# Score products of 64 rows, two heads side by side, issued as one group per chunk with its own rank, in a hybrid decoder trunk

## The chip, the cores and the metric

The kernel runs on one core of a Trainium2 chip. The metric is the device time of one execution in microseconds (us). TensorE is PE in the profile (PEld is its weight load), VectorE DVE, ScalarE ACT, GpSimd POOL, SyncE SP; all loads and stores here are issued from SP's queue.

## The reference

Two layers over 16 meta tokens and 2048 tokens of width 1024, each wrapped in RMSNorms: an even layer (sliding-window attention beside a convolution module) and an odd layer, stick-breaking attention of 16 heads of 64, on which the change lies:

```python
for i in range(nb):
    kend = (i + 1) * BLOCK
    z = jnp.einsum('bqhd,bkhd->bhqk', qp[:, i * BLOCK:kend], kp[:, :kend]).astype(jnp.float32) * scale
    ...
    log_beta = jax.nn.log_sigmoid(z)
    log_1m = jnp.where(valid, jax.nn.log_sigmoid(-z), 0.0)
    after = lax.cumsum(log_1m, axis=3, reverse=True) - log_1m
    a = jnp.where(valid, jnp.exp(log_beta + after), 0.0)
    outs.append(jnp.einsum('bhqk,bkhd->bqhd', a.astype(v.dtype), vp[:, :kend]))
```

A weight is thus the sigmoid of the key's own score, times the product over all later keys of one minus theirs.

## The kernel before

The first part (`layer0`) is the even layer in four chunks of 512 tokens: projections, convolution on DVE, window attention, output projection. Its projections end in PSUM banks that `banks = cycle(BK)` takes in turn from the pools `pj` and `pz`; `pw` (L546) and `outp` (L645) take `pj` alone.

The second part (`layer1`) runs over eight head pairs p, for each the first eight query tiles (`attn(p, 0)`, the first half) and later all of the other eight (`attn(p, 1)`, the second half). `interleave` mixes the steps of `attn` with projection units of another head pair: a unit is 24 products (8 blocks of the width, each in three products of high and low parts, `mm3`, L142 to L144) into one bank. For a pair of query tiles (x = 0, 1) and the two heads (h = 0, 1), `pair_steps` cuts the keys into chunks of at most 512, from the last to the first. One `chunk`:

- For each of four tiles (h, x) the scores `z` (L912): q and k are split into a high and a low part of 64 rows each. The k tile of a head holds both parts above each other (128 rows), the q tile one part twice, so two products of 128 rows give all four terms.
- ACT takes two sigmoids, `om` (L919, of -z) and `be` (L920, of z); POOL masks the diagonal where needed (L923).
- DVE forms the running product of `om` from the right (the scan `S`, L925, that starts from the chunk before) and multiplies `be` by it (L926).
- PE transposes `be` block by block into a bank `pt` (L944), ACT copies it to `aT` (L947 to L950), and PE multiplies by v into `av` (L958), head 0 in the left half of the array's columns and head 1 in the right half. The first `av` of a chunk waits for all copies of the chunk (`after_all`).

The order on each engine is set by a scheduler that takes instructions by rank, normally the order of the code; `high_priority(offset=n)` moves a block n ranks forward (400 for `av`). Each engine then works strictly through its list. A chunk's last `av` is noted in `self.gates`; projections of layer 1 stand behind the fourth last of them (`behind`). The PSUM pools have 2 banks for `pj` (projections), 3 for `pz` (scores), 2 for `pt` and 1 for `av`.

The loads: `start` brings k (four loads per head pair) and v, `qload` brings q for a pair of query tiles (eight loads).

## Time and profile before

| | us |
|---|---|
| median of 3 runs | 2896.34 (2895.69 to 2900.71) |
| profiled execution | 2902.22 |
| its span, first to last instruction | 2900.5 |
| PE busy in the span | 2735.1 |
| DVE busy | 2209.4 |
| ACT busy | 1472.3 |
| scores (L912), 1536 products, busy | 394.9 |

Where the prediction quotes rows: a row of the timeline has start, duration, engine, line, operation, tiles, count, and in brackets the idle time before and what ended it. A group has count | busy time, mean duration in ns of one | idle time before, and its releasers. A row of the waits has who waited, for whom, the total, how often and the longest. A row of stretches has the stretch and its length, then for each engine the busy time and in brackets the instructions, then the granted clock of TensorE, the share of the DMA engines and GB/s. Durations of PE products include their way through the array, so products that follow each other overlap in the record, and a pitch is read from starts or ends.

### The profile page before, as it was taken

How to read it: one execution, taken by the hardware profiler on the slowest of the kernel's cores; microseconds unless marked ns; L12 is line 12 of the kernel's file. 1: busy time of each engine (PE TensorE's matmuls, PEld its weight loads, DVE VectorE, ACT ScalarE, POOL GpSimd, SP SyncE). 2: the span in 40 equal slices, each digit the busy share in tenths (PEclk: the TensorE clock that was granted, in tenths of full speed). 3: DMA queues.
4: the chain of work that ended last, by engine and by line, in shares of the span. 5: the costliest groups of instructions: out<-in, count | busy, mean ns of one | idle time of the engine just before them, and what ended most of it. 6: DMA issues, size and time to landing. Idle time of an engine off the chain costs nothing.

```text
span 2900.5 us, 49605 instructions
## 1 busy us (share of the span) xinstructions
PE 2735.1 (94%) x16110; PEld 2193.5 (76%) x16110; DVE 2209.4 (76%) x3696; ACT 1472.3 (51%) x3574; POOL 777.6 (27%) x2679
## 2 busy tenths in 40 slices
PE   7888999999899999999999899999999999999997
PEld 7886777777688799888887677777777777766876
DVE  7987888888767744666668987878888887887864
ACT  4223434343545323455445656666666766665551
POOL 3431212000000212333335532323223322333210
PEclk9999999999999999999999999999999999999999
DMA  7877888788876664444446462423232342244322
GB/s 258 283 251 221 254 267 256 234 241 267 235 209 187 213 199 146 130 127 137 128 137 182 130 178 65 113 76 101 66 103 88 88 111 73 74 129 126 113 95 91
DMA packets 303986, 462.87 MB, mean 160 GB/s; under 512 B 46640, under 2 KB 200640, under 8 KB 300656
## 3 DMA queue, kind: packets, MB, share of 16 engines
q1 hardware_dynamic: 303728, 459.70, 52.5%
q8 instruction: 129, 2.11, 0.3%
q14 instruction: 129, 1.06, 0.1%
HBM read 312.16 MB, written 142.14 MB: 157 GB/s over the span
## 4 chain that ended last, share of the span: by engine, by line
PE 71%; DVE 10%; DMA 7%; issue 4%; ACT 4%; POOL 2%; SPq 1%; DVEq 0%; ACTq 0%; POOLq 0%
PE pj L142 11%; PE pj L144 11%; PE pj L143 11%; PE z L912 8%; PE av L958 7%; PE pt L944 7%; PE po L142 4%; PE po L144 4%; PE po L143 4%; DVE y L309 3%; DVE S L925 2%; DMA qs<-qr 1%; DVE be L926 1%; DMA raw<-in_w_in 1%; ACT om L919 1%
## 5 line engine op out<-in xcount | busy, mean ns | idle before, releaser
L925 DVE TENSOR_TENSOR_SCAN S<-om,be 128x401 f32<-128x401 f32 (+3 forms) x512 | 536.6, 1069 | 71.9 <-ACT om L919 51.3
L919 ACT ACTIVATE om<-z 128x384 f32<-128x384 f32 (+5 forms) x768 | 377.9, 510 | 196.7 <-PE z L912 131.8
L926 DVE TENSOR_TENSOR be<-be,S 128x385 f32<-128x385 f32 (+5 forms) x768 | 413.6, 563 | 76.0 <-POOL be L917 22.2
L142 PE MATMUL pj<-th,wh 128*128 128x512 f32 (+2 forms) x1280 | 460.5, 360 | 7.1 <-DVE ev L810 3.6
L144 PE MATMUL pj<-th,wl 128*128 128x512 f32 (+2 forms) x1280 | 452.8, 354 | 0.0
L143 PE MATMUL pj<-tl,wh 128*128 128x512 f32 (+2 forms) x1280 | 450.5, 352 | 0.0
L950 ACT COPY aT<-pt 128x512 f32<-128x512 f32 (+2 forms) x672 | 334.2, 504 | 196.6 <-PE pt L944 156.2
L912 PE MATMUL z<-kst,qt 128*128 128x384 f32 (+6 forms) x1536 | 394.9, 357 | 31.2 <-ACT be L920 29.8
L920 ACT ACTIVATE be<-z 128x384 f32<-128x384 f32 (+5 forms) x768 | 375.5, 505 | 72.7 <-PE pt L944 72.0
L309 DVE SCALAR_TENSOR_TENSOR y<-u,cw,y 128x512 f32<-128x512 f32 (+1 forms) x480 | 391.7, 828 | 6.1
L944 PE MATMUL pt<-ident,be 128*128 128x128 f32 x2176 | 363.2, 282 | 17.4 <-ACT ev L799 7.7
L944 PEld LDWEIGHTS pt<-ident,be 128*128 128x128 f32 x2176 | 253.6, 142 | 113.0 <-issue 31.0
L912 PEld LDWEIGHTS z<-kst,qt 128*128 128x128 f32 x1536 | 247.7, 190 | 75.7 <-ACT be L920 55.3
L958 PE MATMUL av<-aT,vt 128*64 128x256 f32 (+1 forms) x2304 | 282.0, 380 | 4.3 <-DVE og L976 4.3
L916 POOL MEMSET om<- 128x1 f32 x768 | 74.8, 99 | 768.6 <-DVE S L925 753.5
L144 PE MATMUL pj<-hTh,wl 128*128 128x512 f32 (+2 forms) x704 | 246.7, 353 | 23.9 <-POOL wl L132 16.9
L142 PEld LDWEIGHTS pj<-th,wh 128*128 128x128 f32 x1280 | 241.8, 189 | 33.9 <-DVE ev L810 4.6
L144 PEld LDWEIGHTS pj<-th,wl 128*128 128x128 f32 x1280 | 241.0, 188 | 29.9
L143 PEld LDWEIGHTS pj<-tl,wh 128*128 128x128 f32 x1280 | 241.4, 189 | 25.1 <-issue 0.4
L142 PE MATMUL pj<-hTh,wh 128*128 128x512 f32 (+2 forms) x704 | 249.6, 356 | 8.9 <-DMA wh<-wk 4.6
L925 DVE TENSOR_TENSOR_SCAN S<-om 128x257 f32<-128x257 f32 (+4 forms) x256 | 204.8, 812 | 63.1 <-POOL om L923 50.3
L143 PE MATMUL pj<-hTl,wh 128*128 128x512 f32 (+2 forms) x704 | 246.8, 351 | 0.8 <-DVE hTl L191 0.8
(184 smaller groups left out, 4702.2 us busy)
## 6 DMA issues: line engine op xcount, KB each, us to landing
raw<-in_w_in SPq DMA_DIRECT2D x98, 512.0 KB, 4.0
wr<-wk SPq DMA_DIRECT2D x44, 512.0 KB, 6.2
wh<-wk SPq DMA_DIRECT2D x44, 512.0 KB, 5.2
wl<-wk SPq DMA_DIRECT2D x44, 512.0 KB, 6.5
qt<-qhd SPq DMA_DIRECT2D x256, 64.0 KB, 2.6
qt<-qld SPq DMA_DIRECT2D x256, 64.0 KB, 2.4
wk<-wh SPq DMA_DIRECT2D x22, 512.0 KB, 4.9
wk<-wl SPq DMA_DIRECT2D x22, 512.0 KB, 4.9
```

The costliest lines, as they stand in the source:

```text
L142: mm(out, sh, mh, start=first, stop=False)
L143: mm(out, sh, ml, start=False, stop=False)
L144: mm(out, sl, mh, start=False, stop=last)
L309: return lambda: nc.vector.scalar_tensor_tensor(y[:, :TC], u[:, w : w + TC], cw[:, j, w : w + 1], y[:, :TC], ALU.mult, ALU.add)
L912: nc.tensor.matmul(z[:, :n], S["q"][2 * h + i][:, x * P : x * P + P], S["k"][h][:, k0 : k0 + n], start=(i == 0), stop=(i == 1))
L919: nc.scalar.activation(om[:, :n], z[:, :n], AF.Sigmoid, scale=-0.125)
L920: nc.scalar.activation(be[:, :n], z[:, :n], AF.Sigmoid, scale=0.125)
L925: nc.vector.tensor_tensor_scan(P_[:, : n + 1][:, ::-1], om[:, : n + 1][:, ::-1], om[:, : n + 1][:, ::-1], init, ALU.mult, ALU.bypass)
L926: nc.vector.tensor_tensor(bl[:, : n + 1], bl[:, : n + 1], P_[:, : n + 1], ALU.mult)
L944: nc.tensor.transpose(pt[:, o : o + P], bes[h, x][:, mo + b * P : mo + b * P + P], self.ident)
L950: cps.append(nc.scalar.copy(aT[:, lo:hi], pt[:, lo:hi]))
L958: mi = nc.tensor.matmul(av[h * HD : h * HD + HD, qc0 + x0 : qc0 + 256], S["v"][:, b0 + b, h * HD : h * HD + HD], at, start=not S["started" ...
```

## The change

The scores become products of 64 rows. The k tiles now hold the high part of both heads above each other, and the low part; q likewise. So head 0 is in rows 0 to 63 and head 1 in rows 64 to 127, and three products (high by high, high by low, low by high) are made for each tile; low by low is left out. All scores of a chunk, up to 12 products into four banks, are issued ahead of its other work, with a rank 800 forward, and the first of them waits for the last sigmoids of the chunk before (`zread[-4:]`) and for the `aT` copies of its head 0 (`half`). The transposes run through head 0 first and then head 1. `pj` has 1 bank and `pz` 4; outside the stretches of attention the projections alternate between both.

```diff
-PB = (2, 3, 2)
+PB = (1, 4, 2)
+ZP = 800
...
-                    ps = self.bank("pj", "pw")
+                    ps = self.bank(next(banks), "pw")
...
+        self.zread, self.half, self.free = [], [], cycle(BK)
...
-                    ps = self.bank("pj", "pj1")
+                    ps = self.bank(next(self.free), "pj1")
...
-                for h in range(2):
+                for i in range(2):
                     kst = w4.tile([P, T], F32R, tag="kst", name="kst")
-                    for i in range(2):
-                        self.mv(kst[i * HD : i * HD + HD, :n], kd[i][p, h * HD : h * HD + HD, :n])
+                    self.mv(kst[:, :n], kd[i][p, :, :n])
                     ks.append(kst)
...
+                for i in range(2):
+                    qt = w2.tile([P, 256], F32R, tag=f"q{i}", name="qt")
+                    self.mv(qt, qd[i][p, :, q0 : q0 + 256])
+                    qs.append(qt)
...
+                    zs, wait = {}, self.zread[-4:] + self.half
+                    for x in range(2):
+                        n = nbs[x] * P + mo
+                        if n == 0:
+                            continue
+                        for h in range(2):
+                            zs[h, x] = self.bank("pz", "z")
+                        with tc.high_priority(offset=ZP):
+                            for i, j in ((0, 0), (0, 1), (1, 0)):
+                                for h in range(2):
+                                    r = slice(h * HD, h * HD + HD)
+                                    mi = nc.tensor.matmul(zs[h, x][:, :n], S["q"][i][r, x * P : x * P + P], S["k"][j][r, k0 : k0 + n], start=(i + j == 0), stop=(i == 1))
+                                    if wait is not None:
+                                        self.after_all(mi, wait)
+                                        wait = None
...
-                            z = self.bank("pz", "z")
-                            for i in range(2):
-                                nc.tensor.matmul(z[:, :n], S["q"][2 * h + i][:, x * P : x * P + P], S["k"][h][:, k0 : k0 + n], start=(i == 0), stop=(i == 1))
+                            z = zs[h, x]
...
-                            nc.scalar.activation(be[:, :n], z[:, :n], AF.Sigmoid, scale=0.125)
+                            self.zread.append(nc.scalar.activation(be[:, :n], z[:, :n], AF.Sigmoid, scale=0.125))
...
-                    for c in range(0, b1 - b0, 2):
-                        cw = min(2, b1 - b0 - c)
-                        aTs = []
-                        for h in range(2):
+                    cps, aTs = [], {}
+                    for h in range(2):
+                        for c in range(0, b1 - b0, 2):
+                            cw = min(2, b1 - b0 - c)
                             pt = self.bank("pt", "pt1")
...
+                        if h == 0:
+                            self.half = cps[:]
...
+        self.free = cycle(("pj",))
         for p in range(2, 6):
             interleave(proj(p, 0), attn(p - 2, 0))
...
+        self.free = cycle(BK)
         for t in range(8, NT):
```

How this moves PE's list in the second half, where three chunks follow each other in head pair 0. Before, the piece has the last transpose for head 0 of a chunk (`be_21300` is its x = 1), then the scores of head 0 for the second chunk after it (`z_21512`, `z_21525`, into whose `be` DVE comes two chunks later), then the `av` of the chunk before, and only then the first transpose of head 1 of the chunk itself (`be_21312`):

```order
L944 MATMUL pt1_21332<-ident_60,be_21300 128x128
L912 MATMUL z_21512<-kst_19877,qt_21102 128x400
L912 MATMUL z_21512<-kst_19877,qt_21105 128x400
L912 MATMUL z_21525<-kst_19877,qt_21102 128x400
L912 MATMUL z_21525<-kst_19877,qt_21105 128x400
L958 MATMUL av1_20627<-aT_21259,vt1_19883 64x256
L958 MATMUL av1_20627<-aT_21266,vt1_19883 64x256
L958 MATMUL av1_20627<-aT_21259,vt1_19883 64x256
L958 MATMUL av1_20627<-aT_21266,vt1_19883 64x256
L958 MATMUL av1_20627<-aT_21271,vt1_19883 64x256
L958 MATMUL av1_20627<-aT_21276,vt1_19883 64x256
L944 MATMUL pt1_21339<-ident_60,be_21312 128x128
```

So the scores of the next chunk were all issued by then, and those of the one after it have begun.

Now, at the same place, the four transposes into the first bank of head 1 of a chunk (`be_21321` is x = 0, `be_21330` is x = 1) stand directly ahead of the scores of the next one, of which these are the first eight (`z_21404` and `z_21412` are head 0, `z_21405` and `z_21413` head 1):

```order
L955 MATMUL pt1_21350<-ident_60,be_21321 128x128
L955 MATMUL pt1_21350<-ident_60,be_21330 128x128
L955 MATMUL pt1_21350<-ident_60,be_21321 128x128
L955 MATMUL pt1_21350<-ident_60,be_21330 128x128
L915 MATMUL z_21404<-kst_19861,qt_21104 128x512
L915 MATMUL z_21405<-kst_19861,qt_21104 128x512
L915 MATMUL z_21412<-kst_19861,qt_21104 128x512
L915 MATMUL z_21413<-kst_19861,qt_21104 128x512
L915 MATMUL z_21404<-kst_19863,qt_21104 128x512
L915 MATMUL z_21412<-kst_19863,qt_21104 128x512
L915 MATMUL z_21405<-kst_19863,qt_21104 128x512
L915 MATMUL z_21413<-kst_19863,qt_21104 128x512
```

No score of the next chunk stands ahead of a transpose that needs the last `be` of this one. The group's first four products alternate between the heads, the rest come by twos.

Right behind them, the last two scores of that group, the rest of head 1's transposes, then a transpose for head 0 of the next chunk (`be_21421`, whose scores are `z_21404`), and the `av` of the chunk itself:

```order
L915 MATMUL z_21405<-kst_19861,qt_21106 128x512
L915 MATMUL z_21413<-kst_19861,qt_21106 128x512
L955 MATMUL pt1_21357<-ident_60,be_21321 128x128
L955 MATMUL pt1_21357<-ident_60,be_21330 128x128
L955 MATMUL pt1_21456<-ident_60,be_21421 128x128
L971 MATMUL av1_20621<-aT_21343,vt1_19865 64x256
L971 MATMUL av1_20621<-aT_21355,vt1_19865 64x256
L971 MATMUL av1_20621<-aT_21343,vt1_19865 64x256
L971 MATMUL av1_20621<-aT_21355,vt1_19865 64x256
L971 MATMUL av1_20621<-aT_21348,vt1_19865 64x256
L971 MATMUL av1_20621<-aT_21360,vt1_19865 64x256
L955 MATMUL pt1_21463<-ident_60,be_21421 128x128
```

The `av` of a chunk has moved behind the first transpose of the next chunk; where a chunk has a projection unit, that too stands behind it, in two parts, ahead of the transposes of head 1.

More of the change, by code (lines that the diff above doesn't have):

```diff
@@ L644, in mm @@
                 w = slice(nh * 512, nh * 512 + 512)
-                ps = self.bank("pj", "po")
+                ps = self.bank(next(banks), "po")
                 for k in range(KB):
@@ L883, in qload @@
                 S["q"] = qs = []
-                for h in range(2):
-                    for i in range(2):
-                        qt = w2.tile([P, 256], F32R, tag=f"q{h}{i}", name="qt")
-                        for j in range(2):
-                            self.mv(qt[j * HD : j * HD + HD], qd[i][p, h * HD : h * HD + HD, q0 : q0 + 256])
-                        qs.append(qt)
+                for i in range(2):
+                    qt = w2.tile([P, 256], F32R, tag=f"q{i}", name="qt")
+                    self.mv(qt, qd[i][p, :, q0 : q0 + 256])
+                    qs.append(qt)
             def pair_steps(m):
@@ L909, in chunk @@
                                 continue
-                            z = self.bank("pz", "z")
-                            for i in range(2):
-                                nc.tensor.matmul(z[:, :n], S["q"][2 * h + i][:, x * P : x * P + P], S["k"][h][:, k0 : k0 + n], start=(i == 0), stop=(i == 1))
+                            z = zs[h, x]
                             om = w3.tile([P, 513], F32, tag="om", name="om")
@@ L930, in chunk @@
                             bes[h, x] = be
-                    cps, avs = [], []
-                    for c in range(0, b1 - b0, 2):
-                        cw = min(2, b1 - b0 - c)
-                        aTs = []
-                        for h in range(2):
+                    cps, aTs = [], {}
+                    for h in range(2):
+                        for c in range(0, b1 - b0, 2):
+                            cw = min(2, b1 - b0 - c)
                             pt = self.bank("pt", "pt1")
@@ L950, in chunk @@
                                 cps.append(nc.scalar.copy(aT[:, lo:hi], pt[:, lo:hi]))
-                            aTs.append(aT)
-                        for b in range(c, c + cw):
-                            o = (b - c) * 256
-                            x0 = 0 if b < nbs[0] else P
-                            avs += [(h, b, x0, aTs[h][:, o + x0 : o + 256]) for h in range(2)]
+                        if h == 0:
+                            self.half = cps[:]
+                    avs = []
+                    for b in range(b1 - b0):
+                        c, x0 = b - b % 2, 0 if b < nbs[0] else P
+                        o = (b - c) * 256
+                        avs += [(h, b, x0, aTs[h, c][:, o + x0 : o + 256]) for h in range(2)]
                     with tc.high_priority(offset=AVP):
@@ L1008, in mm @@
                 w = slice(nh * 512, nh * 512 + 512)
-                ps = self.bank("pj", "po1")
+                ps = self.bank(next(self.free), "po1")
                 for k in range(KB):
```

2 lines of the change are left out of this document (1 added, 1 removed).

## The prediction

> **What bounds the kernel now.** I read the page first (busy shares and the chain that ended last), then the busy time by stage, then the second half of layer 1 by groups and by waits, and last single rows of the timeline for pitches and hand-overs.
>
> ```profile
> span 2900.5 us, 49605 instructions
> PE 2735.1 (94%) x16110; PEld 2193.5 (76%) x16110; DVE 2209.4 (76%) x3696; ACT 1472.3 (51%) x3574; POOL 777.6 (27%) x2679
> PE 71%; DVE 10%; DMA 7%; issue 4%; ACT 4%; POOL 2%; SPq 1%; DVEq 0%; ACTq 0%; POOLq 0%
> ```
>
> The profiled execution took 2902.22 us (span 2900.5), 0.2% above the median of 2896.34; the sum below is made against 2902.22 and 6 us are taken off at the end. TensorE carries the chain. The attention over all 16 query tiles (the second half) is periodic: one head pair, 16 chunks of scores, every 130 us. The stretch below holds six of them, 96 chunks; the second row is one head pair of the first half, 8 chunks.
>
> ```profile
> core 0: us, PE busy (x) PEld busy (x) DVE busy (x) ACT busy (x) POOL busy (x), PEclk, DMA share, GB/s
> 1697.00:2477.00 780.00, 752.57 (x4517) 558.25 (x4517) 647.30 (x844) 525.41 (x1266) 228.59 (x1084) 1.00 0.32 93
> 1217.00:1294.00 77.00, 75.94 (x534) 65.64 (x533) 48.19 (x79) 39.03 (x116) 29.34 (x116) 1.00 0.46 132
> ```
>
> So a chunk of the second half takes 780/96 = 8.13 us, with PE busy 96% and DVE 83%: DVE is close behind. What keeps both busy is that neither waits long for the other. The groups of DVE and the waits in the same 780 us:
>
> ```profile
> L925 DVE TENSOR_TENSOR_SCAN S<-om,be 128x513 f32<-128x513 f32 (+3 forms) x289 | 312.8, 1103 | 40.9 <-ACT om L919 23.2 <-issue 11.6 <-POOL be L917 5.1
> L926 DVE TENSOR_TENSOR be<-be,S 128x385 f32<-128x385 f32 (+3 forms) x385 | 218.8, 597 | 39.6 <-POOL be L917 20.6 <-POOL be L923 7.9 <-POOL am L929 1.8
> L110 DVE TENSOR_TENSOR wl<-raw,wh 128x1024 fp32r<-128x1024 f32 x25 | 30.7, 1226 | 7.8 <-POOL wh L109 7.0 <-POOL be L917 0.5
> L783 DVE TENSOR_TENSOR ev<-pj,ev 128x512 fp32r<-128x512 f32 x24 | 16.6, 690 | 9.5 <-ACT ev L782 9.5
> L810 DVE TENSOR_TENSOR ev<-pj,ev 128x512 f32<-128x512 f32 x13 | 8.9, 684 | 11.2 <-ACT ev L809 11.2
> L976 DVE TENSOR_TENSOR og<-av,g 128x512 f32<-128x512 f32 x12 | 8.3, 688 | 4.7 <-PE av L974 4.7
> DVE S L925 <- ACT om L919: 23.2, 23, 1.7
> PEld z L912 <- ACT be L920: 35.5, 76, 1.2
> PEld pt L944 <- ACT aT L950: 21.8, 78, 0.5
> ```
>
> DVE waited for a score's sigmoid 23 times in 96 chunks, 23.2 us in all: scores are computed one to two chunks before DVE needs them. The other operations of DVE make 30.7 + 16.6 + 8.9 + 8.3 = 64.5 us, which leaves (647.3 - 64.5)/96 = 6.07 us of scans and products for a chunk.
>
> **The change part by part.** Pitches and hand-overs come from these rows:
>
> ```profile
> 1780.82 0.52 PE L912 MATMUL z<-kst,qt 128*128 128x400 f32 x2
> 1781.43 0.51 ACT L919 ACTIVATE om<-z 128x400 f32<-128x400 f32 x1 [1.45 <-PE z L912]
> 1781.97 1.05 DVE L925 TENSOR_TENSOR_SCAN S<-om,be 128x401 f32<-128x401 f32 x1 [1.34 <-ACT om L919]
> 2012.56 0.39 PE L143 MATMUL pj<-tl,wh 128*128 128x512 f32 x1
> 2012.78 0.39 PE L144 MATMUL pj<-th,wl 128*128 128x512 f32 x1
> 2013.01 0.40 PE L142 MATMUL pj<-th,wh 128*128 128x512 f32 x1
> 2004.51 0.60 PE L944 MATMUL pt<-ident,be 128*128 128x128 f32 x4
> 2005.13 0.34 PE L912 MATMUL z<-kst,qt 128*128 128x400 f32 x1
> 2005.40 0.43 PE L958 MATMUL av<-aT,vt 128*64 128x256 f32 x1
> 2005.40 1.30 PE L958 MATMUL av<-aT,vt 128*64 128x256 f32 x12
> 2006.42 0.28 PE L958 MATMUL av<-aT,vt 128*64 128x128 f32 x2
> 2006.63 0.33 PE L944 MATMUL pt<-ident,be 128*128 128x128 f32 x1
> L944 PE MATMUL pt<-ident,be 128*128 128x128 f32 x1196 | 198.4, 280 | 9.3 <-ACT ev L799 4.5 <-ACT aT L950 2.6
> ```
>
> Two scores of 400 columns end 0.52 us after the first starts and one alone lasts 0.34, so a score holds the array for 0.18 us. From the start of the two to ACT's start are 0.61 us, 0.25 more than their 2 x 0.18; from there to DVE's scan 0.54. Projection products start 0.23 apart; four transposes take 0.60 and one 0.28, so 0.107 each. A chunk's `av` products (128*64, a half of the array's columns) take 1.30 for 12. They show what a change of the array's partition costs: the last score ends at 2005.47 and the first `av` at 2005.83, 0.36 later, where the `av` after it take 0.21 (1.30 less 0.43 is 0.87 for three further steps of 0.21 and two of 0.11); on leaving, the last `av` ends at 2006.70 and the next transpose at 2006.96, 0.26 instead of 0.107. So 0.15 us is lost on each crossing.
>
> *Scores of 64 rows.* Before, a chunk had 8 score products, 8 x 0.18 = 1.44 us. Now it has 12 of half the rows. No row shows two row halves at work at once; the bounds are 6 steps (every pair overlaps) and 12 (none does). The order of a group is head 0, 1, 0, 1, then 0, 0, 1, 1 twice; products start in order, and two of one half follow each other, so pairs that overlap make 7 steps. I take 7: 1.26 us, plus two crossings of 0.15, since 128-row transposes stand on both sides: 1.56, so 0.12 us more than before, not less.
>
> [...]
>
> *The hold and the rank.* The first score of a chunk now waits for the sigmoids of the chunk before it and for head 0's `aT` copies. Behind it on PE stand that chunk's last transposes, `av` and the projections. But the order is worse than the wait: PE first transposes head 1 of the chunk before (the order shows it), which needs DVE's last product of that chunk. Then DVE has nothing left when the scores start. A chunk becomes a ring, per mean chunk of the second half:
>  - scores to the first sigmoid: crossing 0.15, five steps (the group's ninth product completes the first bank) 0.90, hand-over 0.25: 1.30;
>  - sigmoid to scan: 0.54;
>  - DVE's four tiles: 6.07;
>  - last product to head 1's transposes to the next scores: three transposes at 0.107 and a hand-over of about 0.13: 0.45.
> Together 8.36 us where PE has no projection to do in the chunk.
>
> Half of the chunks hold a projection unit of 24 products. There PE is the longer way, because the order puts the first transpose of this chunk ahead of the last chunk's `av` and of the unit: it needs 1.30 + 0.54 + one scan 1.05 + one product of 0.58 + 0.05 = 3.52 us after the scores began, and PE has only its 1.56 of scores and about 0.25 of transposes before. Then one transpose 0.11, `av` 1.30 with two crossings 1.60, the unit 24 x 0.23 = 5.52, nine transposes 0.96: 11.71 us.
>
> A head pair has 8 chunks of each kind: 8 x (8.36 + 11.71) = 160.6 instead of 130.0, +30.6. Seven head pairs of the second half run so: +214 us. In the eighth (attention of pair 7 beside the output projection) nearly every chunk has some 25 projection products, several of them ahead of the first transpose:
>
> ```profile
> 2612.00:2815.00 203.00, 196.53 (x1079) 153.81 (x1078) 161.22 (x251) 108.81 (x244) 57.02 (x197) 0.98 0.36 111
> ```
>
> That is 12.7 us per chunk now, and the ring with a unit, 11.71, does not exceed it: 0. In the first half (64 chunks, 9.6 us each in the row above) one or more units stand in most chunks and DVE is busy 63%; there a chunk pays the 0.30 of crossings less a step of 0.13 (270 columns), 11 us, and about a third of the chunks wait some 1 us for their first tile: 20. Together +30; the bounds are 0 and 64 x (3.52 - 1.56) = 125.
>
> *The rest.* q comes in 2 loads per pair of query tiles instead of 8, k in 2 per head pair instead of 4; SP issues less, and before they were hidden: 0, and 2.6 us a pair of tiles if that cover went. The one `pj` bank makes a unit wait for the evacuation of the one before; in the second half a whole chunk lies between two units, in the first half one boundary in 8 chunks is bare, about 1.5 us (0.69 of DVE, the copy and the hand-overs) for each of 6 head pairs, inside the 30. Layer 0 alternates `pj` and `pz` with a unit of 5.5 us between uses of a bank: 0.
>
> ```profile
> qt<-qhd SPq DMA_DIRECT2D x256, 64.0 KB, 2.6
> ```
>
> Sum: 2902 + 214 + 30 = 3146, less 6: **3140 us**.
>
> **Rivals.**
>  1. *The ring is covered and PE's total decides (faster).* If DVE's last product came before PE got to head 1's transposes, PE would only lose 0.12 x 16 = 1.9 us a head pair and win the waits of its loads for sigmoids and copies, (35.5 + 21.8)/6 = 9.6: 7 x 7.7 = 54, so 2842. It decides from the point at which PE's own work in a chunk reaches DVE's way of 8.36 us. For it speaks PE's 96%; against it that without a unit PE has only 3.52 + 0.11 + 1.60 + 0.96 = 6.2.
>  2. *The halves do not overlap.* Then a group takes 12 steps and its first bank nine: 4 x 0.18 = 0.72 on each of 112 rings, 81 us, and 5 x 0.13 on 64 chunks, 42: 3263. Nothing in the profile excludes it. [...]
>  3. *Only chunks without a unit pay.* If PE finds other work while it waits for the first tile, a unit chunk takes 11.71 less the wait 3.52 - 1.81 = 10.0; a pair 146.9; 7 x 16.9 = 118: about 3015.
>
> **How the numbers follow.** Chances: my forecast 0.70, rival 2 0.14, rival 3 0.08, rival 1 0.05, no change for a cause that I don't see 0.03. The forecast's own bounds: first half 0 and units 0.5 shorter, -30 and -28, so 3082; DVE's other 0.67 us a chunk inside the rings without a unit, +38, and 50 more in the first half: 3228. The range goes down to 3060 and up to rival 2, 3265; rivals 1 and 3 lie outside. A difference of 0.2% is about what a measurement of this kernel can tell: faster by more 0.06, within it 0.03, slower by more 0.91.
>
> **What would show it.** Right: in the second half a head pair takes about 160 us; DVE's scan waits for the sigmoid once in every chunk, about 2.3 us; PE's busy share falls to about 80%, its longest waits being transposes for DVE's product; scores stand in groups of 12 whose pairs start together, with gaps of 0.15 at both ends. Wrong: a head pair under 135 us, or a DVE that seldom waits, would refute the ring; scores 0.18 apart without overlap would be rival 2; chunks with a unit near 10 us rival 3.

## The result and the profile after

The changed kernel takes 3395.62 us (median of 4 runs, 3390.51 to 3407.48) beside 2898.53 (median of 4) for the kernel before: a ratio of 1.171 with a 95% interval of 1.167 to 1.176. The forecast was 3140 with a range of 3060 to 3265: right in sign, 256 us too low, outside its range. The profiled execution took 3399.49 us, against 2902.22 before. Its page:

```profile
span 3397.8 us, 50157 instructions
PE 2910.9 (86%) x16878; PEld 2232.6 (66%) x16878; DVE 2216.9 (65%) x3696; ACT 1456.2 (43%) x3568; POOL 776.8 (23%) x2679
PEclk9999999999999999999888988888888989888999
PE 33%; DVE 8%; ACT 6%; issue 4%; POOL 1%; DMA 1%; SPq 0%; DVEq 0%; ACTq 0%; POOLq 0%
```

DVE has the same work as before (2209.4 us there) in 497 us more of span, so DVE waits. PE is busy 176 us longer with fewer steps of scores, and the slices of the clock point to why: 8s appear where every slice was a 9 before (granted clock over the span 0.928, before 0.982). The next two rows are the stretches of three head pairs of the first half and of five head pairs (80 chunks) of the second half, each from the first scan of a pair to the first scan of a later one:

```profile
1178.10:1461.40 283.30, 245.64 (x1691) 196.37 (x1690) 147.77 (x237) 115.27 (x345) 90.11 (x349) 0.97 0.30 96
1995.10:2910.70 915.60, 721.45 (x4090) 499.33 (x4090) 543.89 (x702) 438.58 (x1053) 184.16 (x903) 0.87 0.18 59
```

A head pair takes 94.4 us in the first half (77 before) and 183.1 in the second (130 before). PE is busy 79% there, DVE 59%, and the clock granted to PE is 0.87 where it was 1.00. The waits in these 80 chunks (who waits, for whom, total, times, longest):

```profile
PE pt L955 <- DVE be L938: 134.6, 84, 2.4
DVE S L937 <- ACT om L931: 119.6, 45, 5.7
DVE ev L785 <- ACT ev L784: 99.0, 18, 7.0
DVE ev L812 <- ACT ev L811: 44.4, 10, 5.7
DVE S L937 <- POOL be L929: 40.6, 17, 4.3
PE av L971 <- ACT aT L961: 38.0, 31, 2.2
DVE S L937 <- POOL om L935: 14.4, 5, 4.0
```

Before, all waits of DVE's scans made 48.7 us in 80 chunks, 0.6 us a chunk (20.0 of it for a sigmoid); now they make 119.6 + 40.6 + 14.4 = 174.6 us, 2.2 us a chunk. DVE waits a further 143.4 us where an evacuation of a projection unit (`ev`) stands in its list, and PE's longest waits are transposes for DVE's product. One ring of a chunk without a projection unit, at full clock (granted 1.00 from 2841.26 to 2850.18), in order of time (rows of the three engines, the first and the last step of each):

```profile
2841.26 1.36 PE L915 MATMUL z<-kst,qt 64*128 64x400 f32 x12
2842.51 0.51 ACT L931 ACTIVATE om<-z 128x400 f32<-128x400 f32 x1 [0.55 <-PE z L915]
...
2843.12 1.05 DVE L937 TENSOR_TENSOR_SCAN S<-om,be 128x401 f32<-128x401 f32 x1 [3.35 <-ACT om L931]
...
2844.83 0.64 ACT L961 COPY aT<-pt 128x512 f32<-128x512 f32 x1
...
2845.53 1.95 PE L971 MATMUL av<-aT,vt 128*64 128x256 f32 x16 [2.20 <-ACT aT L961]
...
2848.81 0.58 DVE L938 TENSOR_TENSOR be<-be,S 128x401 f32<-128x401 f32 x1
...
2850.18 0.39 PE L915 MATMUL z<-kst,qt 64*128 64x256 f32 x2
```

From the start of the scores to the first sigmoid 1.25 us, to the scan 0.61, from there to the end of the last product (2849.39) 6.27, to the next scores 0.79: 8.92 us. The ring is there as forecast (1.30 + 0.54 + 6.07 + 0.45). In the same chunk a second wait shows that the forecast did not have: `av` starts 4.27 us after the scores, because the copy it needs (2844.83) stands on ACT behind six sigmoids of the new chunk.

Where the difference lies, from the starts of the scans in both traces:

| | before | after | difference | forecast |
|---|---|---|---|---|
| up to layer 1's first scan | 1068.1 | 1085.3 | +17 | 0 |
| eight head pairs, first half | 635.2 | 732.1 | +97 | +30 |
| pairs 0 to 5, second half | 777.8 | 1093.3 | +316 | +184 |
| pair 6 | 137.3 | 201.5 | +64 | +31 |
| pair 7 | 192.4 | 199.5 | +7 | 0 |
| rest of the span | 89.7 | 86.2 | -3 | 0 |

### The profile page after: what moved, and what is told of

It is laid out like the page before. It is cut to its first block, busy times and chain, and to the rows that moved or that the text cites. A ratio compares the mean times of both kernels' runs of the same rounds, so it can differ in the third digit from the quotient of the medians.

```text
span 3397.8 us, 50157 instructions
## 1 busy us (share of the span) xinstructions
PE 2910.9 (86%) x16878; PEld 2232.6 (66%) x16878; DVE 2216.9 (65%) x3696; ACT 1456.2 (43%) x3568; POOL 776.8 (23%) x2679
## 4 chain that ended last, share of the span: by engine, by line
PE 33%; DVE 8%; ACT 6%; issue 4%; POOL 1%; DMA 1%; SPq 0%; DVEq 0%; ACTq 0%; POOLq 0%
PE av L971 7%; PE pt L955 5%; PE z L915 4%; DVE S L937 4%; PE pj L143 4%; PE pj L144 4%; PE pj L145 4%; ACT be L932 3%; DVE be L938 2%; ACT om L931 2%; PE po L143 2%; PE po L145 2%; PE po L144 2%; ACT aT L961 1%; DVE wl L111 1%
## 5 line engine op out<-in xcount | busy, mean ns | idle before, releaser
L955 PE MATMUL pt<-ident,be 128*128 128x128 f32 x2176 | 445.1, 314 | 301.2 <-DVE be L938 239.8
L955 PEld LDWEIGHTS pt<-ident,be 128*128 128x128 f32 x2176 | 278.4, 154 | 493.6 <-issue 263.8
L961 ACT COPY aT<-pt 128x512 f32<-128x512 f32 (+2 forms) x672 | 322.0, 509 | 537.4 <-PE pt L955 529.6
L931 ACT ACTIVATE om<-z 128x384 f32<-128x384 f32 (+5 forms) x768 | 387.9, 506 | 302.3 <-PE z L915 273.7
L143 PE MATMUL pj<-th,wh 128*128 128x512 f32 (+2 forms) x1280 | 476.8, 373 | 20.1 <-DVE ev L785 11.6
L971 PE MATMUL av<-aT,vt 128*64 128x256 f32 (+1 forms) x2304 | 346.0, 446 | 70.0 <-ACT aT L961 66.2
L932 ACT ACTIVATE be<-z 128x384 f32<-128x384 f32 (+5 forms) x768 | 393.1, 513 | 0.0
L971 PEld LDWEIGHTS av<-aT,vt 128*64 128x64 f32 x2304 | 172.8, 158 | 188.5 <-ACT aT L961 90.5
L143 PEld LDWEIGHTS pj<-th,wh 128*128 128x128 f32 x1280 | 252.7, 197 | 64.9 <-DVE ev L785 14.8
L915 PE MATMUL z<-kst,qt 64*128 64x384 f32 (+6 forms) x2304 | 272.0, 372 | 4.0 <-ACT aT L961 2.5
L145 PE MATMUL pj<-hTh,wl 128*128 128x512 f32 (+2 forms) x704 | 244.1, 350 | 13.2 <-POOL wl L133 12.0
```

The lines of the kernel that those rows point to most:

```text
L143: mm(out, sh, mh, start=first, stop=False)
L145: mm(out, sl, mh, start=False, stop=last)
L915: mi = nc.tensor.matmul(zs[h, x][:, :n], S["q"][i][r, x * P : x * P + P], S["k"][j][r, k0 : k0 + n], start=(i + j == 0), stop=(i == 1))
L931: nc.scalar.activation(om[:, :n], z[:, :n], AF.Sigmoid, scale=-0.125)
L932: self.zread.append(nc.scalar.activation(be[:, :n], z[:, :n], AF.Sigmoid, scale=0.125))
L955: nc.tensor.transpose(pt[:, o : o + P], bes[h, x][:, mo + b * P : mo + b * P + P], self.ident)
```

## The experiments

Theory: the order and the hold close a ring through DVE. Rivals: the products of 64 rows and their crossings cost the time; the one projection bank does; the rank does; PE's lower clock does. Each run has its ratio to the kernel before, measured beside it, with the 95% interval. Rows of stretches are again three head pairs of the first half or five of the second, so a length is divided by 3 or 5. Where a chunk's time is given, the second half of pairs 0 to 5 was cut at each start of a group of scores, and the chunks with no projection product and those with 20 to 28 were averaged: in the change 9.85 us (48 chunks) and 12.98 us (47, without the very first). The 16 chunks of a pair differ in size, so a mean over some of them depends on which they are; the same chunk of another pair (the ninth, say) has the same size and nearly the same projection work.

### The hold opened

```
-                    zs, wait = {}, self.zread[-4:] + self.half
+                    zs, wait = {}, self.zread[-4:]
```

> The changed kernel, but the first score of a chunk waits only for the last sigmoids of the chunk before, no longer for its head 0 copies. In the order its 12 products then stand ahead of head 1's transposes of the chunk two before and ahead of head 0's transposes of the chunk before, so one chunk of scores lies in front of DVE. Ring theory (the order closes a ring scores, sigmoid, DVE, head 1's transposes, next scores): the ring opens, a head pair of the second half falls from 182 us to 125 to 132, the first half back to about 77, total 2840 to 2910. Row theory (products of 64 rows and their crossings cost the time): no more than 100 us of the 500 come back, total over 3250. Bank theory (one bank for the projections costs the first half its 100 us): second half as in the ring theory, but the first half keeps about 93 us a pair, total 2950 to 3000.

3046.64 us, ratio 1.051 (1.049 to 1.053). Three head pairs of the first half and five of the second:

```profile
1166.70:1422.00 255.30, 236.96 (x1692) 191.10 (x1689) 148.58 (x238) 115.75 (x346) 84.69 (x349) 0.99 0.34 107
1890.10:2610.70 720.60, 628.59 (x4092) 449.49 (x4091) 545.72 (x700) 439.66 (x1050) 191.94 (x901) 0.97 0.22 74
```

Its longest waits of DVE and of PE in the second of these stretches:

```profile
DVE S L937 <- ACT om L931: 118.3, 45, 5.0
PE pt L955 <- ACT aT L961: 54.1, 45, 1.7
DVE S L937 <- POOL om L935: 25.1, 15, 4.4
```

The one added wait for head 0's copies, with the order that the scheduler makes of it, costs 349 of the 497 us: a head pair falls from 183.1 to 144.1 in the second half and from 94.4 to 85.1 in the first. But no theory had the total: 14 us a pair remain. PE's wait for DVE's product is gone; in its place PE waits for copies (54 us). The scans of DVE still wait 144 us in 80 chunks, 1.8 us each, so a scan that waits is no mark of the ring; PE's wait for DVE's product is.

### Products of 128 rows under the same hold and rank

The loads of k and q and the two products of a tile are those of before:

```
-                            for i, j in ((0, 0), (0, 1), (1, 0)):
-                                for h in range(2):
...
+                            for h in range(2):
+                                for i in range(2):
...
```

> The changed kernel with the score products of before: two of 128 rows for a tile, k and q loaded as before, all eight of a chunk in one group with the same hold and rank. Ring theory: the eight products take 8 x 0.18 = 1.44 us instead of about 1.2 and the crossings of 0.3 fall away, the ring stays: 3340 to 3420. Row theory: back to 2900 to 3000.

3342.86 us, ratio 1.154 (1.151 to 1.156); a head pair takes 96.8 in the first half and in the second 171.6, from this stretch of five:

```profile
1987.80:2845.80 858.00, 676.46 (x3772) 500.34 (x3771) 542.54 (x701) 434.22 (x1051) 183.70 (x901) 0.94 0.24 68
```

The ring stays without any product of 64 rows, so the row theory falls as the main cause. In the ring the change with its 64 rows is 53 us slower all the same, a part of which can be the clock (0.87 against 0.94 here): with 128 rows the first sigmoid starts 0.65 to 0.97 us after the scores, with 64 rows 1.12 to 1.52 (means for chunks with and without a unit, with and without half clock), since five of the six steps stand ahead of it.

### Products of 64 rows alone, without a partner

```
-                            for i in range(2):
-                                nc.tensor.matmul(z[:, :n], S["q"][2 * h + i][:, x * P : x * P + P], S["k"][h][:, k0 : k0 + n], start=(i == 0), stop=(i == 1))
+                            r = slice(h * HD, h * HD + HD)
+                            for i, j in ((0, 0), (0, 1), (1, 0)):
+                                nc.tensor.matmul(z[:, :n], S["q"][i][r, x * P : x * P + P], S["k"][j][r, k0 : k0 + n], start=(i + j == 0), stop=(i == 1))
```

> The kernel before with only the score products changed: three of 64 rows for each tile, one tile after the other as before, so that no product has a partner in the other half; no hold, no rank, banks as before. If a product of half the rows holds the array as long as one of 128 and each entry and exit costs 0.15: 12 steps instead of 8, +0.72 us a chunk, and some three groups of scores a chunk with 0.3 each, +0.9: 1.6 us on 128 chunks and 1.4 on 64, total 3150 to 3220. If the crossings are hidden: about 3030. If the 0.72 too fits into the waits of PE (4% of 8.13 us is 0.3): no lower than 2960.

3128.97 us, ratio 1.078 (1.076 to 1.080); 152.9 a pair in the second half, 85.5 in the first. The five pairs of the second half:

```profile
1908.90:2673.20 764.30, 750.67 (x4092) 517.70 (x4091) 544.55 (x702) 456.93 (x1050) 185.41 (x901) 0.99 0.21 70
```

And from the timeline the three products of one tile, and what follows:

```profile
2101.26 0.79 PE L910 MATMUL z<-kst,qt 64*128 64x384 f32 x3
2101.99 0.66 PE L942 MATMUL pt<-ident,be 128*128 128x128 f32 x4
```

PE is busy 98%: without a ring, but with 12 steps, the kernel is bound by PE. Three products take 0.79 us where one lasts 0.34, so half the rows save nothing when no partner runs beside them. The total is 21 us under the expected 3150.

### The banks alone

```
-PB = (2, 3, 2)
+PB = (1, 4, 2)
...
-                    ps = self.bank("pj", "pj1")
+                    ps = self.bank(next(self.free), "pj1")
```

> The kernel before with only the banks of the change: one for the projections of layer 1 beside attention, four for scores, projections elsewhere in turn from both. Bank theory: the first half goes from 77 to about 93 us a head pair, total 2980 to 3010. Ring theory: a bare evacuation of about 1.5 us at one boundary in eight chunks, total 2895 to 2925.

2918.91 us, ratio 1.006 (1.004 to 1.009). A head pair takes 79.3 in the first half and 134.8 in the second, but pair 7 takes 169.9 instead of 192.4. In the kernel before, the banks are a small part, as the ring theory had it.

### No hold at all

```
-                    zs, wait = {}, self.zread[-4:] + self.half
+                    zs, wait = {}, None
```

> The changed kernel without any added wait in front of the scores; rank 800 stays. In the order most scores then stand as three products of one tile (609 groups of three against 72 of six), so that partners in the two halves no longer meet; they run one to two chunks ahead. Ring theory: no ring, but 12 steps and more crossings as in the run with rows of 64 alone (154 us a head pair): 3050 to 3150. If the rank itself, and not the hold, is what costs: well over 3150.

3139.25 us, ratio 1.083 (1.081 to 1.084).

Five pairs of the second half:

```profile
1920.20:2674.60 754.40, 747.13 (x4096) 502.66 (x4092) 546.46 (x701) 452.70 (x1051) 186.25 (x901) 1.00 0.21 71
```

150.9 us a pair, PE busy 99% at full clock: the ring is gone, and the partners with it. So a hold has a use: it makes the four tiles of a chunk ready together, so that both halves get products in turn. Of the change's two waits the one for the sigmoids does that; the one for head 0's copies only closes the ring.

### The rank taken away

```
-ZP = 800
+ZP = 0
```

> The changed kernel with the rank 0 instead of 800; the hold stays, and the order still puts the scores of a chunk behind head 1's transposes of the chunk before, now behind nearly all of them. Ring theory: the hold makes the ring, so as slow or slower than the change: 3370 to 3480. Rank theory (scores of the highest rank push transposes and projections back): faster by over 100 us.

3330.21 us, ratio 1.149 (1.147 to 1.151): 65 us faster than the change, where the ring theory had said no faster. A head pair of the second half takes 177.6; the stretch of five:

```profile
1960.40:2848.30 887.90, 737.20 (x4094) 517.95 (x4092) 536.92 (x701) 438.03 (x1052) 193.60 (x902) 0.83 0.18 60
```

The order now puts the `av` products, and most of a unit, ahead of the first transpose of the next chunk. Five of the 16 chunks of a pair have a unit and run at full clock in both kernels: they take 10.5 us on average here and 12.2 in the change. So the prediction's third rival, near 10.0, comes about in these chunks of this kernel; over all chunks with a unit the means are 12.0 and 13.0, at a clock that is lower here. The chunks without a unit take 10.15 us (9.85 in the change), and PE still waits 103.1 us for DVE's product: the ring stays.

### Pairs in groups of six

A group is one query tile of both heads and waits for its own two banks; the rank is 400:

```
-ZP = 800
+ZP = 400
...
-                    zs, wait = {}, self.zread[-4:] + self.half
+                    zs, wait = {}, None
...
+                        wait = [self.zsig[i] for i in (len(self.zal) - 4, len(self.zal) - 3) if i >= 0]
                         for h in range(2):
                             zs[h, x] = self.bank("pz", "z")
+                            self.zal.append((h, x))
...
```

> Products of 64 rows of two heads side by side, but in groups of six (one query tile, two banks), each held only until its own two banks have been read, with rank 400 and the other lines as in the change. In the order 341 groups of six stand one chunk ahead, two in a chunk at different places. If the whole-chunk group of four banks is what is left after the hold is opened: 3 steps of 0.18 and 0.30 of crossings twice a chunk, 1.68 us against 1.44 before; a head pair 128 to 138 us, total 2870 to 2960. If products of 64 rows or the banks cost the rest: about 144 us as with the hold opened, 3020 to 3060.

3011.09 us, ratio 1.039 (1.038 to 1.041), between the two expectations. The second half is as expected, 136.4 us a pair at a clock of 1.00; the first is not, 92.1. The stretches of three and five pairs:

```profile
1168.10:1444.50 276.40, 246.77 (x1691) 201.27 (x1690) 152.17 (x238) 116.44 (x345) 90.17 (x349) 0.96 0.31 99
1897.80:2579.90 682.10, 627.52 (x4092) 436.78 (x4092) 537.03 (x700) 447.66 (x1051) 188.75 (x901) 1.00 0.24 78
```

A row of the waits in the first of them:

```profile
PE pj L143 <- DVE ev L785: 23.4, 9, 3.6
```

The next unit waits 7.8 us a pair for the one projection bank, whose evacuation stands on DVE behind scans.

### Work in PE's waits

```
+                            if c == 0:
+                                for _ in range(12):
+                                    nc.tensor.transpose(pt[:, 256:384], self.ident, self.ident)
```

> The changed kernel with 12 extra transposes of the identity matrix ahead of the first transposes of each head in each chunk (their values are overwritten or not read): work for TensorE at the two places where it waits for DVE, 1.28 us each at full clock. Ring theory: the waits are the time, half clock only a few tenths of it; the half-clock time falls from 490 us to under 200, a chunk without a unit goes from 9.85 to about 9.5 us, one with a unit from 13.0 to 13.0 to 13.6 since the fill ahead of head 1 is not covered there: total 3360 to 3440. Clock theory (the granted clock made the 256 us that the forecast missed): a chunk without a unit goes to about 8.4 us and the total to under 3300.

3593.79 us, ratio 1.239 (1.238 to 1.241): 198 us more than the change, far outside every expectation. The five pairs of the second half, and the fill's own wait there:

```profile
2072.20:3075.70 1003.50, 864.88 (x6010) 673.40 (x6010) 541.09 (x701) 436.68 (x1051) 188.43 (x902) 0.97 0.16 54
```

```profile
PE pt L951 <- ACT aT L964: 75.2, 70, 2.1
```

The clock went from 0.87 to 0.97, but the fill was no free work: it waited for its bank to be copied, and what stood behind it waited too. A chunk without a unit went up to 11.4 us. So this run does not show the clock's price.

### The kernel before with paired products

```
+                        wait = [self.zsig[i] for i in (len(self.zsig) - 3, len(self.zsig) - 2) if i >= 0]
+                        zs = [self.bank("pz", "z") for h in range(2)]
+                        with tc.high_priority(offset=ZP):
+                            for i, j in ((0, 0), (0, 1), (1, 0)):
+                                for h in range(2):
...
```

> The kernel before with one thing of the change, the products of 64 rows of two heads side by side, in groups of six (one query tile at a time: both heads' scores, sigmoids, scans and products, then the other tile). A group waits only until the two of the three score banks that it takes have been read; rank 200; banks and transposes as before. The order has two groups of six in a chunk, one chunk ahead. Row theory turned round (paired products are cheaper, the hold and the banks cost): a group 3 steps and 0.30, about 1.55 us a chunk as in the run of pairs instead of 1.87 with the waits of before, so a head pair of the second half 125 to 131 us, of the first half 75 to 80, total 2850 to 2920. If the pairs themselves cost: as in the run of pairs, 136 and 92, total near 3000.

2963.58 us, ratio 1.022 (1.019 to 1.025), slower than expected: 79.9 us a pair in the first half and 134.0 in the second. The five pairs there, and PE's longest wait in them:

```profile
1859.40:2529.60 670.20, 631.69 (x4094) 436.19 (x4092) 542.51 (x701) 440.62 (x1050) 190.61 (x902) 1.00 0.24 80
```

```profile
PE z L914 <- ACT be L927: 24.6, 36, 1.1
```

PE is busy 631.69 us in 80 chunks, where the kernel before needs 627.1 (752.57 in 96 chunks, the row in the prediction): so the two steps saved in a chunk (0.36) bring nothing; the crossings of two groups are the likely price. And PE waits for sigmoids, 24.6 us in 80 chunks (14.0 before), where a group needs two banks at once.

### The pairs with the banks of before

The run of pairs, with:

```
-PB = (1, 4, 2)
+PB = (2, 3, 2)
```

and with one query tile's scores, sigmoids, scans and products ahead of the other's, and rank 200.

> The run of pairs with the banks of before (two for projections, three for scores), so with one query tile's scores and sigmoids after the other; transposes head by head as in the change. If the one projection bank made the first half 92 us a pair there: back to 76 to 82. Second half 130 to 137, total 2890 to 2970. If the order of the transposes costs it: first half still about 90.

3021.14 us, ratio 1.041 (1.039 to 1.043). First half 79.3 us a pair, second 140.5, pair 7 229.6. The stretches of three and of five pairs:

```profile
1195.30:1433.10 237.80, 235.22 (x1676) 188.74 (x1670) 148.46 (x236) 116.68 (x345) 80.69 (x348) 1.00 0.36 112
1866.30:2568.80 702.50, 636.35 (x4094) 441.76 (x4092) 544.58 (x700) 445.31 (x1052) 196.88 (x902) 0.98 0.23 76
```

The first half is back at 79.3 from 92.1, and PE's wait for the projection bank (7.8 us a pair) is gone from it. That much is the one projection bank; rank and order changed too, so the other 5 us are not told apart. The total is above the expected 2970, since the second half is slower by 4 us a pair than with four score banks, and pair 7 by 70.

### The hold opened, with 128 rows

> The run without the wait for head 0's copies, with the products of 128 rows of before. Its scores stand in groups of eight, one chunk ahead as there. 8 steps of 0.18 are 1.44 us against 1.30 measured there with the crossings: a head pair 144 to 148, total 3030 to 3090. If products of 64 rows and their crossings make part of the 14 us by which a pair stands above the kernel before: under 3010.

The edit is those of the first two runs together. 3024.37 us, ratio 1.042 (1.040 to 1.045), just under the expected range; 141.2 us a pair in the second half, from this stretch:

```profile
1890.80:2596.70 705.90, 631.10 (x3773) 482.33 (x3772) 536.02 (x701) 441.66 (x1051) 196.33 (x901) 0.98 0.29 83
```

The same hold with 64 rows took 144.1 and in total 22 us more: the paired products, with fewer steps, bring nothing here. The runs now make a chain for a head pair of the second half, each with more of the change than the one before it: the kernel before 129.9; the banks 134.8; the group of four banks with its rank, its wait for the sigmoids and the new order of transposes 141.2; the products of 64 rows 144.1; the wait for head 0's copies 183.1. That is 4.9, 6.4, 2.9 and 39.0.

### More work in DVE's chain

```
+                            nc.vector.tensor_tensor(P_[:, : n + 1], P_[:, : n + 1], P_[:, : n + 1], ALU.max)
```

> The changed kernel with one more DVE operation in each tile's chain, between the scan and the product (the maximum of the scan with itself, which leaves the values as they are): about 0.56 us a tile, 2.24 a chunk. Ring theory: a chunk without a unit takes all of it, 9.85 becomes 12.1. In the order the last chunk's products by v, and part of a unit, now stand ahead of the next chunk's first transpose, so a chunk with a unit stays at 11.5 to 13.5; a head pair 187 to 205, total 3420 to 3590. If PE's own work at its lower clock sets the chunk (DVE is busy 65% of the span): a chunk without a unit gains under 1 us.

3596.54 us, ratio 1.239 (1.237 to 1.242); 204.9 us a pair, at the upper edge of the expectation, and the total 7 us over it. The five pairs:

```profile
2049.40:3073.90 1024.50, 763.00 (x4090) 522.08 (x4090) 692.75 (x1022) 438.12 (x1053) 193.82 (x904) 0.82 0.16 52
```

DVE's busy time rose by 692.75 - 543.89 = 148.9 us in 80 chunks, 1.86 each (not the estimated 2.24), and a chunk without a unit by 1.82, from 9.85 to 11.67. DVE is busy only 68% of this stretch, yet nearly all of what is put into it comes out as time of the chunk: it lies on the ring. The clock fell too, from 0.87 to 0.82, so a part of the 1.82 can be the clock. A chunk with a unit went to 14.0, above the expected 13.5.

### Work in the wait ahead of head 0's transposes only

```
+                            if c == 0 and h == 0:
+                                for _ in range(12):
+                                    nc.tensor.transpose(pt[:, 256:384], self.ident, self.ident)
```

> The changed kernel with the 12 extra transposes of the identity matrix ahead of head 0's first transposes only, where PE waits about 1.7 us in every chunk for the first tile; nothing is added ahead of head 1, where the extra work of the other run stood in DVE's way. If half clock costs only what the chunks of the trace show beside each other (9.85 against 9.54 us without a unit, 12.98 against 12.31 with one): about 1.0 us less for two chunks, 8 us a head pair, total 3330 to 3390, with half-clock time well under 490 us. If half clock makes most of what the forecast missed: a head pair near 165 us, total under 3290. If the fill runs late and pushes the transposes back: over 3400.

3404.83 us, ratio 1.174 (1.171 to 1.178): the time of the change, and by the expectation just in its third case. Five pairs of the second half:

```profile
1991.20:2915.60 924.40, 767.07 (x5050) 568.92 (x5050) 542.72 (x701) 436.74 (x1052) 185.88 (x903) 0.96 0.18 58
```

The fill's own wait there:

```profile
PE pt L951 <- ACT aT L964: 43.2, 20, 2.6
```

Over the span the granted clock is 0.972 against 0.928. In the slow stretches of the change it is 0.50 (from 2192.41 to 2206.05 us, for one); with 0.50 here too that is (1 - 0.928) x 2 x 3397.8 = 489 us of half clock in the change and 191 here. 300 us of half clock are gone and the time is no shorter; but the fill has a price of its own, so this does not show that half clock was cheap. At full clock in both kernels, the 9th chunk of a pair takes 14.25 us here and 12.82 in the change, the 11th 10.23 and 8.92, the 12th 13.88 and 12.62. What the clock gave and what the fill took are read apart below.

## Why the prediction was right in sign and wrong in size

**The ring: right, with one term too small.** Its marks came as named: PE is busy 79% (80% forecast), its longest waits are transposes for DVE's product, and DVE's scans wait 2.2 us a chunk (2.3), though this last mark proves little, since they wait 1.8 us with the ring opened too. Over all 48 chunks without a unit the parts are, measured against forecast: scores to first sigmoid 1.45 (1.30), sigmoid to scan 0.68 (0.54), DVE's four tiles 6.74 (6.07), last product to next scores 0.99 (0.45); together 9.85 against 8.36. The term that failed is "DVE's four tiles: 6.07". It was a mean over all chunks, put into those without a unit; but a mean over a mixed stretch is no duration of a kind of chunk. The chunks without a unit are the larger ones: their four tiles have 1752 columns of scores on average, those of the chunks with a unit 1484. From first scan to last product the former take 6.74 and the latter 6.12. The forecast's own bound for DVE's other work, +38, was of this size by luck: no other work of DVE lies between these scans and products in any of the 48 chunks. The run with more DVE work shows that this term counts nearly one for one.

**A chunk with a unit: 12.98 against 11.71.** The forecast let PE wait for the first tile ahead of the first transpose and then run through. The trace shows a second wait ahead of `av`, whose copies stand on ACT behind sigmoids of the next chunk: 38.0 us in 80 chunks, of which 24.9 in the 40 chunks with a unit, 0.62 us each. With the hold opened this wait is 17.0 us and with rank 0 it is 0.8; no run moved the copies alone, so its share in the 1.27 is read from the trace, not shown.

**Half clock: not foreseen.** Everything was costed at full clock, which the trace before granted (1.00 in the rows of both halves in the prediction, 0.98 in its row beside the output projection). In the change PE's work lasts about 1.85 times as long in places, here at a granted clock of 0.50 (2192.41 to 2206.05):

```profile
2199.89 1.11 PE L955 MATMUL pt<-ident,be 128*128 128x128 f32 x4
2202.68 3.59 PE L971 MATMUL av<-aT,vt 128*64 128x256 f32 x16
```

Four transposes take 0.60 at full clock, and the 16 `av` took 1.95 in the ring above. What this costs shows best where the same chunk of different pairs runs with half clock and without, in the trace of the change. The 13th chunk, with a unit, takes 11.66 to 11.69 us at full clock and 13.20 to 13.23 at a granted clock of 0.87; the 11th, without one, 8.91 to 8.93 at full clock and 10.24 to 10.60 at 0.83 to 0.84; but the 10th takes 10.27 at full clock and 10.27 to 10.46 at 0.83 to 0.84. Each of these slower chunks has about 3.4 us at half clock, as (1 - 0.87) x 2 x 13.2 gives. So half clock cost them from nothing to about half of the time that it lasted.

Ten of the 16 chunks of a pair occur at full clock in the change, and against these the means stand 4.8 us a pair too high. The other six never do; against the last run, which has them at full clock, they stand 5.4 too high, in part by a single chunk. So by this estimate half clock makes about 10 of the 22 us a pair between 160.6 and 182.6. The other 12 are at full clock: the DVE term above (8 x 0.67 = 5.4) and the wait ahead of `av` (8 x 0.62 = 5.0) are of that size together. The 9.54 and 12.31 of the expectation of the last run are means of just those chunks that happen to run at full clock (six and 28), which are not of the average size, so the 8 us a pair worked out there was not well founded.

The trace has 232 us at half clock in these five pairs, a mean of 0.87. If each of them cost half of itself, that would be 23 us a pair; the chunks give about 10. No wait of PE in these 80 chunks is longer than 2.4 us; what brings PE to half clock was not shown.

**Rival 2, that the halves do not overlap: refuted, and the 7 steps were one too many.** All six products of each half stand one step behind the other, and those of the two halves start together (3 to 19 ns apart in the group of 2841.26), also where the order has two of one half in a row, as is read from the number of steps: the group of 400 columns lasts 1.29 us from its start to the next transposes (2842.56), which is six steps of 0.18 and 0.21 more at its two ends. The forecast had 1.56. At 384 columns the twelve products take 1.32 us in the change (2128.27), and three without a partner 0.79 in the run of 64 rows alone. The term was too dear, and it hardly matters: on the ring lies only the part of the group up to the first sigmoid, and that came out at 1.45 instead of 1.30.

**Rivals 1 and 3.** With the hold opened the ring closes no more, yet the time does not fall under that of before: the 2842 of rival 1 was not reached by any of the 13 kernels, the nearest being the banks alone, 2918.91. Rival 3 does not happen in the change; with rank 0 it does in the chunks with a unit that run at full clock.

**The first half: +97 instead of +30.** Per pair 94.4 against 76.5. The hold makes 9.3 of it (85.1 without). The banks alone cost 2.8 in the order of before. In the run of pairs PE waited 7.8 us a pair for the one projection bank, and that wait is gone in the run with two: a bare evacuation was costed at 1.5 us "inside the 30", and what was left out is that the evacuation stands on DVE behind scans. In the change itself PE waits only 2.2 us a pair for evacuations (6.5 in three pairs), and 8.0 for copies and for DVE's product (9.0 + 8.1 + 6.9 in three). So the bank is a small part of its 18 us; what makes the rest beside the hold was not tested.

**Layer 0, pair 6 and pair 7.** Forecast 0, 31 and 0; measured 17, 64 and 7. Layer 0 went up by the same order in the run of the banks alone (28 us up to the first scan), where the first pair then took 61 us less; so it is partly work that moves over the border. Why pair 6 pays twice a ring was not tested.

In short, the step that failed is the price of a pass through the ring: its DVE term was too small for the chunks it was used for, the wait ahead of `av` was missing, and half clock was put at nothing. What stays open: no run took away half clock, or the wait ahead of `av`, and nothing else, so their shares of the 22 us a pair are estimates; and pair 6.

## What to carry to other kernels

Before adding a wait, write down the loop that it closes, and ask of each engine in it whether it has anything left to do while the loop runs; a hold that groups work is useful only up to the point at which the group is ready. Cost such a loop with durations of the very kind of pass that runs it, not with a mean over all passes. And where the change makes the busiest engine wait, count with its clock too: here half clock cost a chunk from nothing to about half of the time that it lasted (0 to 1.7 us for about 3.4 us). Work put into the waits to keep the clock up is not free either; compare the same pass with and without it.

## What the runs showed of the hardware

- The two row halves of the array work as two streams: in the group shown above (2841.26) partners start 3 to 19 ns apart, and 12 products, of which the order has two of one half in a row, take six steps.
- In the run of 64 rows alone three products of 384 columns without a partner take 0.79 us, 0.45 more than the 0.34 of one, which is two steps; scores of 128 rows start 0.18 apart at this width in the kernel before. In the change the next end comes 0.26 us later where such a group is left for 128-row transposes, against 0.11 behind scores of 128 rows in the kernel before. On entry behind transposes the first pitch is 0.28 instead of 0.18, but scores of 128 rows have 0.26 there as well; behind projection products it is 0.28 (the change, 3166.96) against 0.18 (before).
- PE fell to half clock in the 80 chunks of the change with no wait over 2.4 us. Over five head pairs of the second half the granted clock was 1.00 with PE busy 97% (before), 0.97 with 87% (the hold opened), 0.87 with 79% (the change) and 0.82 with 74% (more work in DVE's chain). But 79% went with 0.94 as well (128 rows under the same hold), and 83% with 0.83 (rank 0) and with 0.96 (work ahead of head 0's transposes): the busy share of the stretch alone does not tell the clock.
